# The head of a hybrid trunk's first mixer: three modulation sums on TensorE, a first group in halves, and projections whose sums stay in PSUM over two or three groups

## The chip, the cores and the metric

The kernel runs on one core of one Trainium2 chip. The metric is the device time of one execution in microseconds (us). Before the change three runs took 2713.58, 2715.54 and 2716.81; their median is 2715.54.

## The reference, cut to what matters

Two layers, 256 tokens, 2048 features, all in float32. The change touches the part from the input to the projections of layer 0's mixer:

```
c_act = silu(c)
mod   = c_act @ mod_w[layer] + mod_b[layer]        # 2048 x 12288 per layer
sh1, sc1, g1, sh2, sc2, g2 = split(mod, 6)
h     = rms_norm(x, norm_mix_w) * (1 + sc1) + sh1
proj  = h @ w_in                                   # layer 0: 2048 x 7184
gq, gk, gv, gz, gb, ga, aq, ak, av = split(proj)   # each 1024 wide, gb and ga 8
o_a = gated_deltanet(gq, gk, gv, gz, gb, ga, ...)  # causal conv of 4 taps and silu on q, k, v; l2 norm of q, k
o_b = chunk_band_attention(aq, ak, av, ...)        # rms norm of q and k per head
x   = x + g1 * (concat(o_a, o_b) @ w_out)          # then an MLP, then layer 1 (an SSD mixer and an MLP)
```

## The kernel before, in words

Activations lie feature-major in SBUF: 128 features on the partitions, 256 tokens along the free axis. The 2048 features are four groups `kg` of 4 x 128 rows. A weight chunk is 512 rows by 512 columns (1 MB), and a projection block is finished once its chunks of all four groups have been summed in PSUM.

A float32 product goes through TensorE in one of two ways. In a split chunk ScalarE rounds the weights to `wh` (L317) and VectorE takes the rest `wl` (L321), each in two halves of 128 x 1024, and each tile takes three fast products, wh·u_hi, wh·u_lo and wl·u_hi. In a whole chunk the raw float32 weights meet the float32 activations `hw` (L867); every such product stands as two records in the trace. Blocks that the gated delta rule uses (q, k, v: GQ, GK, GV, called q0, q1 and so on for the first and second 512 columns) have 256-column products with the weights stationary (`b_item`). Blocks for attention (AQ, AK, AV) have 512-column products with the activations stationary (`a_item`).

The head (L1543 to 1580) loads x, squares it on ScalarE, adds the squares on VectorE in eleven steps of 256 columns (L833), and gets the sum over features with ten one-column products against ones (20 records). Scale and shift of layer 0's first norm come from `mod_job`: one row of 128 outputs by 2048 inputs (1 MB) is loaded, and one VectorE instruction multiplies it with the broadcast silu(c) (`crow`) and sums it (L439). For the first group eight rows are needed, four feature blocks of 128 in both kinds. `norm_unit` then makes x·scale·R (`hf`, L862, VectorE), adds the shift and rounds (L864, ScalarE), and takes the rest (L865, VectorE).

Groups 0 to 2 each run eight chunks: k0 and q0, whose sums stay in PSUM banks (`pm`) over all groups, and v0, k1, q1, v1, aq, ak, whose sums leave PSUM after each group into SBUF (`partial`): copied by ScalarE in group 0 (L1590), added by VectorE in groups 1 and 2 (L1592). Meanwhile eight modulation rows per group go through VectorE. Group 3 runs k0, q0, the four chunks of AV, v0, the gates (`n_item`), and aq, ak, k1, q1, v1 whole; behind each block its convolution or head norm follows, and behind the gates the delta rule of the first heads (`gdn_group`) in small products that lie between the chunks. AQ+1, AK+1, AV+1, GZ and GZ+1 follow, four chunks each.

What sets the order: the program is written with short generator tasks. `tick` runs tasks between products by credits, `pump` issues modulation rows at `rate` per step, and a list scheduler of the framework then orders each engine's instructions by its own priorities, except where `keep_in_program_order` pins one. [...] All weight and modulation loads are issued by SyncE, in order, into four buffers of 1 MB (`rawp`); split halves have four buffers each (`wp`); units `up` are 18 of 4 KB per partition; PSUM has four single banks (`pm`) and two pairs (`pg`).

Of the kernel before, what the change touches and what calls it, by code (L numbers as in the profile page):

```python
# [112 lines left out]
class Trunk:  # L113
# [8 lines left out]
    def __init__(self, tc, ctx, ins, out):  # L122
# [7 lines left out]
        self.u_p = pool("up", 18)  # L130
# [9 lines left out]
        self.ahead = []  # L140
        self.pin_mod = 0
# [196 lines left out]
    def constants(self):  # L338
# [7 lines left out]
        cact = self.const([P, 16], "cact")  # L346
# [21 lines left out]
    def constants2(self):  # L368
# [3 lines left out]
        for n, f in (("gconv", 0.5), ("gnw", 0.5), ("sconv", 0.5), ("sconv_b", 0.5), ("qnw", P ** -0.5)):  # L372
            nc.vector.tensor_scalar(col(n), col(n), f, None, op0=ALU.mult)
# [50 lines left out]

    def mod_job(self, layer, vs, fs, step):


        nc = self.nc
        key = ("mix", layer) if vs[0] < 3 else ("mlp", layer)
        for f0 in range(fs.start, fs.stop, step):  # L430
            s = slice(f0, f0 + step)
            for f in range(f0, f0 + step):
                for v in vs:
                    t = self.mod[v % 3, key]
                    raw = self.raw_p.tile([P, 2048], F32, tag="raw", name=self.nm("mraw"))
                    nc.sync.dma_start(raw, self.i["mod"][layer, v, f])
                    yield
                    with self.priority(20):
                        x = nc.vector.scalar_tensor_tensor(raw, raw, 1.0, self.crow, op0=ALU.mult, op1=ALU.mult, accum_out=t[:, f : f + 1])  # L439
                    if self.pin_mod > 0:  # L440
                        self.pin_mod -= 1
                        self.tc.keep_in_program_order(x)
                    if f < s.stop - 1 or v != vs[-1]:
                        yield
            for v in vs:
                t = self.mod[v % 3, key][:, s]
                nc.vector.tensor_tensor(t, t, self.modb[:, layer, v, s], op=ALU.add)
                if v % 3 == 1:
                    nc.vector.scalar_tensor_tensor(t, t, 1.0, self.nw[key][:, s], op0=ALU.add, op1=ALU.mult)
                self.ready[v % 3, key] = f0 + step  # L450
# [22 lines left out]
    def loader(self, src, whole=False):  # L473
# [4 lines left out]
        res = []  # L478

        def load():  # L480
            raw = self.raw_p.tile([P, 2048], F32, tag="raw", name=self.nm("raw"))
            nc.sync.dma_start(raw, src)
            for hf in range(2):
                r = raw[:, 1024 * hf : 1024 * hf + 1024]
# [16 lines left out]
    def b_item(self, ps, src, act, first, last, after=None, whole=False):  # L501

        load, ws = self.loader(src, whole)

        def run():
            o_, (u, x) = ps(), act()
            for hf, (wh, wl) in enumerate(self.tiles(ws, 512)):
# [301 lines left out]
    def sumsq(self, cb, b, late=False):  # L809
# [3 lines left out]
        x = self.x[cb][:, 2 * b : 2 * b + 2]  # L813
        if cb == 3:
# [34 lines left out]
    def norm_unit(self, r, cb, key, acts, whole=False):  # L849
# [4 lines left out]
        x = []  # L854
        for b in range(2):
            h = self.s2([P, 2, SEQ], tag="hf")
            if whole:
                x.append(self.s2([P, 2, SEQ], tag="hw"))
            for f in range(2):
# [372 lines left out]
    def att_qk(self, ps, nw, part=None):  # L1232
# [19 lines left out]
        res = self.unit()  # L1252
# [284 lines left out]
    def run(self):  # L1537
# [274 lines left out]
```

## Time and profile before

| | us |
|---|---|
| median of the runs | 2715.54 |
| the profiled execution | 2719.37 |
| its span in the trace | 2717.6 |
| PE busy in the span | 2665.0 (98%) |
| DVE busy | 2147.6 (79%) |
| ACT busy | 1351.2 (50%) |

The profiled execution is 3.8 us above the median. PE is TensorE's matmuls, PEld its weight loads, DVE VectorE, ACT ScalarE, SP SyncE. A tile's name is given without its buffer number; `mraw` is a modulation row, `raw` a weight chunk, `u` a unit. Each row of a timeline gives start, duration, engine, source line, operation, output and inputs, shapes, count, and in brackets the idle time before it with what ended it.

### The profile page before, as it was taken

To read this page: it belongs to the slowest core of one execution; us is meant where nothing else is said; L and a number is where in the kernel's file an instruction comes from. 1 tells how busy PE (TensorE), PEld (TensorE's weight loads), DVE (VectorE), ACT (ScalarE), POOL (GpSimd) and SP (SyncE) were. 2 spreads that over 40 slices of the span, in tenths; PEclk is the share of its full clock that TensorE was granted. 3 is DMA by queue.
4 is the path that set the end of the run, shared out by engine and by line. 5 is a ranking of instruction groups with operands and counts; after the bars stand their busy time and mean duration, and the time that the engine had idled before them with its cause. 6 is when DMAs were issued, how large, how long until landed. Compare 5 with 4: busy or idle time off the path is not lost.

```text
span 2717.6 us, 39677 instructions
## 1 busy us (share of the span) xinstructions
PE 2665.0 (98%) x15664; PEld 2350.4 (86%) x15664; DVE 2147.6 (79%) x3081; ACT 1351.2 (50%) x1976; POOL 24.5 (1%) x98
## 2 busy tenths in 40 slices
PE   5999999999999999999999999999999999999999
PEld 5887989888888888888888888888888888888888
DVE  7998998987888888889889876897777855555554
ACT  3444454546445354454556544665555354454452
POOL 1000000000000000000000000000000000000000
PEclk9999999999999999999999999999999999999999
DMA  9986487867899898988456665554558855555554
GB/s 341 353 325 235 172 301 272 294 241 282 322 339 328 328 336 330 333 331 307 165 185 217 217 234 200 203 185 172 196 177 293 324 201 188 188 191 193 186 192 134
DMA packets 100459, 680.06 MB, mean 250 GB/s; under 512 B 11185, under 2 KB 14513, under 8 KB 19377
## 3 DMA queue, kind: packets, MB, share of 16 engines
q1 hardware_dynamic: 95376, 669.07, 68.5%
q10 hardware_dynamic: 4896, 8.46, 1.0%
q8 instruction: 123, 2.02, 0.3%
q14 instruction: 64, 0.52, 0.1%
HBM read 675.33 MB, written 2.16 MB: 249 GB/s over the span
## 4 chain that ended last, share of the span: by engine, by line
PE 90%; DVE 6%; DMA 1%; ACT 1%; issue 1%; SPq 0%; ACTq 0%; DVEq 0%
PE pw L308 70%; PE pg L308 13%; PE pm L311 4%; PE pm L308 3%; DVE mraw L439 2%; DVE wl L321 1%; PE pm L314 1%; DMA mraw<-in_mod_dram 1%; DVE u L1592 0%; ACT wh L317 0%; DVE hf L862 0%; ACT pm L1042 0%; DMA raw<-in_w_ab_dram 0%; DMA x<-in_x_dram 0%; DVE u L865 0%
## 5 line engine op out<-in xcount | busy, mean ns | idle before, releaser
L317 ACT CAST wh<-raw 128x1024 fp32r<-128x1024 f32 x870 | 907.1, 1051 | 1031.6 <-PE pw L308 732.9
L321 DVE TENSOR_TENSOR wl<-raw,wh 128x1024 fp32r<-128x1024 f32 x870 | 1048.7, 1220 | 463.8 <-ACT wh L317 349.6
L308 PE MATMUL pw<-u,wh 128*128 128x512 f32 x5584 | 1321.6, 391 | 2.6 <-DVE pad L973 1.9
L308 PEld LDWEIGHTS pw<-u,wh 128*128 128x128 f32 x5584 | 1032.2, 188 | 208.2 <-issue 3.3
L308 PEld LDWEIGHTS pw<-u,wl 128*128 128x128 f32 x5584 | 702.3, 191 | 21.3 <-issue 2.1
L308 PE MATMUL pw<-u,wl 128*128 128x256 f32 x5584 | 714.5, 283 | 0.3 <-DVE wl L321 0.3
L439 DVE SCALAR_TENSOR_TENSOR mraw<-mraw,crow 128x2048 f32<-128x2048 f32 x192 | 438.0, 2283 | 17.8 <-DMA mraw<-in_mod_dram 17.5
L308 PE MATMUL pg<-wh,u 128*128 128x512 f32 x864 | 281.6, 397 | 0.0
L308 PEld LDWEIGHTS pg<-wh,u 128*128 128x128 f32 x864 | 161.9, 188 | 32.1 <-issue 0.5
L925 DVE SCALAR_TENSOR_TENSOR x<-pw,mod,x 128x256 f32<-128x256 f32 x352 | 161.1, 478 | 22.6 <-PE pw L308 20.3
L308 PE MATMUL pg<-wl,u 128*128 128x512 f32 x432 | 169.9, 393 | 0.7 <-DVE wl L321 0.5
L308 PE MATMUL pg<-u,wh 128*128 128x256 f32 x672 | 124.6, 285 | 0.0
L308 PEld LDWEIGHTS pg<-u,wh 128*128 128x128 f32 x672 | 105.7, 192 | 0.3
L308 PEld LDWEIGHTS pg<-wl,u 128*128 128x128 f32 x432 | 81.4, 188 | 17.6 <-DVE wl L321 2.1
L308 PE MATMUL pg<-u,wl 128*128 128x256 f32 x336 | 95.3, 284 | 0.0
L308 PE MATMUL pm<-u,wh 128*128 128x256 f32 (+1 forms) x304 | 64.6, 310 | 19.2 <-ACT wh L317 19.2
L308 PEld LDWEIGHTS pm<-u,wh 128*128 128x128 f32 x304 | 49.1, 198 | 20.3 <-ACT wh L317 20.0
L308 PEld LDWEIGHTS pg<-u,wl 128*128 128x128 f32 x336 | 64.4, 192 | 0.1
L984 DVE SCALAR_TENSOR_TENSOR u<-pad,cst,u 128x256 f32<-128x256 f32 x144 | 60.6, 477 | 3.3 <-ACT u L978 3.2
L864 ACT ACTIVATE u<-hf,mod 128x256 fp32r<-128x256 f32 x64 | 29.3, 502 | 53.0 <-DVE hf L862 53.0
L1504 ACT ACTIVATE rl<-rs 128x512 f32<-128x512 f32 x64 | 40.4, 632 | 18.9 <-DVE rs L1499 14.4
L308 PE MATMUL pm<-u,wl 128*128 128x256 f32 x176 | 46.1, 290 | 3.1 <-DVE wl L321 3.1
(299 smaller groups left out, 1580.5 us busy)
## 6 DMA issues: line engine op xcount, KB each, us to landing
raw<-in_w_dram SPq DMA_DIRECT2D x256, 1024.0 KB, 5.0
mraw<-in_mod_dram SPq DMA_DIRECT2D x192, 1024.0 KB, 6.0
raw<-in_w_ab_dram SPq DMA_DIRECT2D x56, 1024.0 KB, 5.7
raw<-in_w_ssd_dram SPq DMA_DIRECT2D x48, 1024.0 KB, 4.9
raw<-in_w_sz_dram SPq DMA_DIRECT2D x32, 1024.0 KB, 4.9
raw<-in_wo_ssd_dram SPq DMA_DIRECT2D x32, 1024.0 KB, 4.8
raw<-in_wo_ab_dram SPq DMA_DIRECT2D x16, 1024.0 KB, 5.2
sE<-sd_rowd ACTq DMA_DIRECT2D x32, 256.0 KB, 4.9
```

Source lines behind the costliest of these rows:

```text
L308: self.nc.tensor.matmul(o, a, b, start=start, stop=stop, skip_group_check=True)
L311: self.nc.tensor.matmul(o, lhsT, rhs, start=True, stop=True, skip_group_check=True)
L314: self.nc.tensor.transpose(o, a, self.ident[:k, :k])
L317: a = self.nc.scalar.copy(hi, src)
L321: b = self.nc.vector.tensor_tensor(lo, src, hi.bitcast(F32), op=ALU.subtract)
L439: x = nc.vector.scalar_tensor_tensor(raw, raw, 1.0, self.crow, op0=ALU.mult, op1=ALU.mult, accum_out=t[:, f : f + 1])
L864: nc.scalar.activation(hi, h[:, f], AF.Identity, bias=shift[:, col])
L925: nc.vector.scalar_tensor_tensor(x[:, 2 * b + f], ps[:, f, n], g[:, 2 * cb + f : 2 * cb + f + 1], x[:, 2 * b + f], op0=ALU.mult, op1=ALU.add)
L984: nc.vector.scalar_tensor_tensor(h, pad[:, f, 1 + q : 257 + q], w[:, q, j : j + 1], h, op0=ALU.mult, op1=ALU.add)
L1504: nc.scalar.activation(rl, lo, AF.Relu)
```

## The change

Eight things change, all in the first mixer's part of `run` and in its helpers.

1. Three of the first eight modulation sums (shift and scale of feature group 0, shift of group 2) become TensorE products (`mod_pe`): the row arrives in another layout (a new input `mod0`, the same numbers), and 16 products of a 128 x 128 slice with one column of silu(c) give the 128 sums in a PSUM column of `sums`. `mod_fin` adds the bias from there. The other five stay on VectorE.
2. The squares are added in seven steps of 512 columns (L846), and four ones-products are left of ten.
3. `norm_first` replaces `norm_unit` for the mixer's norm: x·R over 512 columns on VectorE (L893), scale and shift in one ScalarE instruction per 256 columns (L902), then rounding and rest over 512 columns. The float32 result exists in every group, so any group can have whole chunks.
4. Group 0 begins in halves: the first half of k0 whole, then halves of q0, v0, k1 with the first half of the unit; the second halves follow once the modulation columns 2 and 3 are there. Half chunks are loaded into units, which are 19 instead of 18.
5. Instead of six blocks copied or added per group, each block's sums stay in PSUM for one, two or three groups, and are copied out once by ScalarE. The 24 VectorE additions of L1592 are gone; four additions come later, where a block's copied sum meets its last one.
6. The chunks are in another order (below). The chunks with k0's first half, aq of group 1, av of group 2 and k0 of group 3 become whole beside the five that were.
7. `rate` is 0.67, 0.57 and 0.57 instead of 0.5 in groups 0 to 2.
8. The head's loads and some small instructions are pinned in program order.

Order of the chunks before, with the group behind the @ and W for whole:

```
@0, @1, @2: k0 q0 v0 k1 q1 v1 aq ak
@3: k0 q0 | AV@0-3 | v0 | gates | aqW akW | (delta rule 0) | k1W | (attention 0) | q1W v1W | AQ+1@0-3 | (delta rule 1) | AK+1@0-3 ...
```

And now:

```
0: k0W(half) q0(half) v0(half) k1(half) | v0 k1 k0 q0 (second halves) | q1@0 v1@0 aq@0 ak@0
1: aqW@1 ak@1 k0@1 q0@1 av@0 av@1 aq1@0 aq1@1
2: avW@2 aq1@2 k0@2 q0@2 v0@1 v0@2 k1@1 k1@2
3: k0W q0 v0 | gates | k1W | aq@2 aqW@3 | (delta rule 0) | ak@2 akW@3 | av@3 | q1@1 q1@2 q1W@3 | (attention 0) | v1@1 v1@2 v1W@3 | aq1@3 | (delta rule 1) | AK+1@0-3 ...
```

```diff
+    def mod_pe(self, raw, o):
+        for k in range(16):
+            self.mmx(o, raw[:, k * P : k * P + P], self.cact[:, k : k + 1], k == 0, k == 15)
+
+    def mod_fin(self, layer, v, s, src=None):
+        key = ("mix", layer) if v < 3 else ("mlp", layer)
+        nc, t = self.nc, self.mod[v % 3, key][:, s]
+        a = nc.vector.tensor_tensor(t, t if src is None else src, self.modb[:, layer, v, s], op=ALU.add)
+        if self.in_order == 2:
+            self.tc.keep_in_program_order(a)
...
+    def norm_first(self, cb, key, acts, now=False):
+        nc = self.nc
+        scale, shift = self.mod[1, key], self.mod[0, key]
+        p, x = self.pair(), [self.s2([P, 2, SEQ], tag="hw") for _ in range(2)]
...
+            a = nc.vector.tensor_tensor(x[b], self.x[cb][:, 2 * b : 2 * b + 2], self.row(self.R, 2), op=ALU.mult)
...
+                nc.scalar.activation(x[b][:, f], x[b][:, f], AF.Identity, scale=scale[:, col], bias=shift[:, col])
+            self.split(x[b], p[b][:, :, 0], p[b][:, :, 1])
...
+        self.mod_pe(pe0, sums[:, 0:1])
...
+        self.mod_sum(dv0, 0, 0, 1)
+        r = self.norm_r()
+        self.pin_mod = 1
+        self.mod_sum(dv1, 0, 1, 1)
+        self.mod_pe(pe1, sums[:, 1:2])
+        nc.scalar.copy(self.R, self.norm_bc(r))
...
         def partial(n, ps):
-            first = parts[n] is None
-            if first:
-                parts[n] = self.unit(shape=[P, 2, 512])
+            parts[n] = self.unit(shape=[P, 2, 512])
             for b in range(2):
-                o = ps[b].rearrange("p f t -> p (f t)") if len(ps[b].shape) == 3 else ps[b]
-                if first:
-                    nc.scalar.copy(parts[n][:, b], o)
-                else:
-                    nc.vector.tensor_tensor(parts[n][:, b], o, parts[n][:, b], op=ALU.add)
+                nc.scalar.copy(parts[n][:, b], ps[b].rearrange("p f t -> p (f t)") if len(ps[b].shape) == 3 else ps[b])
...
+        chunk("k0", 0, True, (0,))
+        chunk("q0", 0, False, (0,))
+        self.mod_sum(dv[0], 0, 1, 2)
+        self.constants2()
+        self.mod_pe(pe2, sums[:, 2:3])
+        chunk("v0", 0, False, (0,))
+        dv = [self.mod_load(mod[0, v, 3]) for v in range(2)]
+        self.mod_fin(0, 0, slice(2, 3), sums[:, 2:3])
...
+        group(0, [("v0", 0, False), ("k1", 0, False), ("k0", 0, True), ("q0", 0, True),
+                  ("q1", 0, False), ("v1", 0, False), ("aq", 0, True), ("ak", 0, True)])
```

How this moves instructions, first on TensorE at the start. The rows are the engine's list in order; `ones,sq` are the sums of squares, `ident,rsy` the norm's broadcast, `cact,mraw` a modulation sum, `hw,u` the whole half of k0 (its weights are in a unit), `u,wh` and `u,wl` split products. Before:

```order
L308 MATMUL pm_163<-ones,ss 128x1 x2
L308 MATMUL pm_163<-ones,sq_162 128x1 x4
L308 MATMUL pm_163<-ones,sq_172 128x1 x4
L314 MATMUL pm_205<-ident,rsy_191 128x128 x2
L308 MATMUL pm_315<-u_289,wh_231 128x256 x2
L308 MATMUL pm_316<-u_289,wh_231 128x256 x2
L308 MATMUL pm_315<-u_289,wl_232 128x256
```

And of the changed kernel:

```order
L309 MATMUL pm_135<-cact,mraw_136 128x1 x16
L309 MATMUL pm_188<-ones,sq_185 128x1 x4
L309 MATMUL pm_135<-cact,mraw_144 128x1 x16
L315 MATMUL pm_227<-ident,rsy_196 128x128 x2
L309 MATMUL pm_299<-hw_233,u_236 128x256 x4
L309 MATMUL pm_300<-hw_233,u_236 128x256 x4
L309 MATMUL pm_135<-cact,mraw_289 128x1 x16
L309 MATMUL pm_341<-u_231,wh_295 128x256 x2
```

Two modulation sums stand ahead of the broadcast, and the third between the first and the second half chunk.

VectorE behind that third sum, in the changed kernel: `pm_135` is the PSUM tile of the three sums, wl_296 belongs to q0's half, wl_338 to v0's, wl_377 to k1's.

```order
L322 TENSOR_TENSOR wl_296<-u_293,wh_295 128x1024
L377 TENSOR_SCALAR cst<-cst 128x8
L377 TENSOR_SCALAR cst<-cst 128x64
L447 TENSOR_TENSOR mod_123<-pm_135,cst 128x1
L447 TENSOR_TENSOR mod_124<-mod_124,cst 128x1
L451 SCALAR_TENSOR_TENSOR mod_124<-mod_124,cst 128x1
L322 TENSOR_TENSOR wl_338<-u_335,wh_337 128x1024
L434 SCALAR_TENSOR_TENSOR mraw_367,mod_123<-mraw_367,crow 128x2048
```

The bias addition that reads the third sum stands ahead of v0's and k1's splits and of two more modulation rows.

TensorE in group 3, around the first delta rule's products. `gu` makes the decay matrices, `pm<-u` and `pm<-u,u` are small products of the convolved k and q, `hw,raw` and `raw,hw` are whole chunks, `wh,u` and `wl,u` split ones, `ident,…` transposes. Before (k1's whole chunk is pg_2568, q1's pg_2705):

```order
L311 MATMUL pm_2453<-gu_2411,SUmask 128x512
L314 MATMUL pm_2458<-ident,u_2154 128x128 x4
L314 MATMUL pm_2465<-ident,u_2154 128x128 x4
L311 MATMUL pm_2493<-u_1843 128x128 x4
L311 MATMUL pm_2506<-u_1843 128x128 x4
L311 MATMUL pm_2519<-u_1926,u_1843 128x128 x4
L308 MATMUL pg_2568<-hw_1718,raw_2339 128x256 x8
L308 MATMUL pg_2568<-hw_1728,raw_2339 128x256 x5
L311 MATMUL pm_2526<-u_1926,u_1843 128x128 x4
L308 MATMUL pg_2568<-hw_1728,raw_2339 128x256 x3
L308 MATMUL pg_2705<-hw_1718,raw_2560 128x256 x6
```

And of the changed kernel, where pg_2087 is ak and pg_2346 av:

```order
L312 MATMUL pm_2166<-gu_2128,SUmask 128x512
L315 MATMUL pm_2183<-ident,u_496 128x128 x4
L315 MATMUL pm_2190<-ident,u_496 128x128 x4
L312 MATMUL pm_2220<-u_1683 128x128 x4
L312 MATMUL pm_2233<-u_1683 128x128 x4
L309 MATMUL pg_2087<-raw_2085,hw_1313 128x512
L309 MATMUL pg_2346<-wh_2250,u_1310 128x512
L309 MATMUL pg_2346<-wl_2251,u_1310 128x512
```

Where a whole chunk followed the small products, a split one follows now, whose wl_2251 and wl_2255 VectorE makes inside the delta rule's chain.

## Rows read from the trace of the kernel before

**Rows 1.** The page: chain that ended last, by engine.

```profile
PE 90%; DVE 6%; DMA 1%; ACT 1%; issue 1%; SPq 0%; ACTq 0%; DVEq 0%
```

**Rows 2.** Stretches of the head, groups 0 to 2, and group 3's first two parts.

```profile
core 0: us, PE busy (x) PEld busy (x) DVE busy (x) ACT busy (x) POOL busy (x), PEclk, DMA share, GB/s
0.00:40.16 40.16, 8.71 (x38) 7.91 (x38) 29.06 (x60) 10.76 (x22) 8.33 (x38) 1.00 0.93 351
40.16:90.20 50.04, 48.29 (x337) 45.76 (x337) 40.97 (x49) 22.90 (x33) 0.00 (x0) 1.00 0.94 342
90.20:138.80 48.60, 46.95 (x341) 44.15 (x342) 46.89 (x56) 19.57 (x23) 0.00 (x0) 1.00 0.93 345
138.80:187.43 48.63, 46.48 (x336) 43.52 (x337) 47.61 (x60) 19.78 (x25) 0.00 (x0) 1.00 0.94 348
187.43:236.90 49.47, 49.47 (x286) 41.19 (x286) 47.74 (x74) 24.23 (x40) 0.62 (x6) 1.00 0.69 253
236.90:290.00 53.10, 52.34 (x306) 42.96 (x305) 46.56 (x152) 29.64 (x112) 3.42 (x10) 1.00 0.51 187
```

**Rows 3.** PE in order of time, the head.

```profile
5.50 3.65 PE L314 MATMUL pm<-ident,cact 128*128 128x128 f32 x16 [5.50 <-DVE cact L349]
...
22.03 0.66 PE L314 MATMUL pm<-ident,rsy 128*128 128x128 f32 x2 [6.63 <-DVE rsy L276]
40.16 1.22 PE L308 MATMUL pm<-u,wh 128*128 128x256 f32 x4 [17.47 <-ACT wh L317]
```

**Rows 4.** The chain in order of time: start, length, engine and line.

```profile
2.17 6.27 DMA x<-in_x_dram
9.19 0.47 ACT crow L358
11.01 4.41 PE pm L308 x20
...
30.89 4.43 DVE mraw L439 x4
...
89.10 1.04 ACT wh L317
90.16 1.24 DVE wl L321
```

**Rows 5.** Stretches whose records are of one kind (columns as rows 2).

```profile
11.01:15.40 4.39, 4.39 (x20) 4.31 (x20) 0.00 (x0) 0.71 (x2) 0.00 (x0) 1.00 1.02 426
40.16:45.21 5.05, 5.01 (x21) 4.72 (x22) 5.05 (x7) 3.43 (x6) 0.00 (x0) 1.00 0.81 290
45.21:60.00 14.79, 14.79 (x123) 14.79 (x123) 11.65 (x12) 4.20 (x4) 0.00 (x0) 1.00 1.00 351
198.57:220.36 21.79, 21.79 (x99) 18.03 (x97) 21.79 (x33) 11.66 (x18) 0.31 (x3) 1.00 0.60 205
427.80:431.30 3.50, 3.36 (x16) 3.39 (x17) 2.26 (x4) 1.65 (x3) 0.00 (x0) 0.51 0.95 365
```

**Rows 6.** PE later: whole chunks, a one-column product, two waits.

```profile
187.43 0.39 PE L308 MATMUL pm<-u,wl 128*128 128x256 f32 x1 [1.01 <-DVE wl L321]
229.75 7.03 PE L308 MATMUL pg<-raw,hw 128*128 128x512 f32 x16
245.88 4.05 PE L308 MATMUL pg<-hw,raw 128*128 128x256 f32 x18
575.16 0.50 PE L308 MATMUL pm<-ones,sq 128*128 128x1 f32 x4
427.94 1.09 PE L314 MATMUL pm<-ident,aq 128*128 128x128 f32 x4 [2.02 <-DVE aq L1250]
```

**Rows 7.** Groups of instructions from 40.16 to 187.43: busy, mean ns, idle before.

```profile
L321 DVE TENSOR_TENSOR wl<-raw,wh 128x1024 fp32r<-128x1024 f32 x49 | 57.9, 1219 | 9.9 <-ACT wh L317 9.5 <-issue 0.3
L439 DVE SCALAR_TENSOR_TENSOR mraw<-mraw,crow 128x2048 f32<-128x2048 f32 x24 | 54.8, 2282 | 0.2 <-DMA mraw<-in_mod_dram 0.2
L1592 DVE TENSOR_TENSOR u<-pg,u 128x512 f32<-128x512 f32 x22 | 14.3, 682 | 0.9 <-PE pg L308 0.9
L864 ACT ACTIVATE u<-hf,mod 128x256 fp32r<-128x256 f32 x13 | 6.5, 508 | 16.0 <-DVE hf L862 16.0
L447 DVE TENSOR_TENSOR mod<-mod,cst 128x2 f32<-128x2 f32 x12 | 1.9, 158 | 0.3
```

**Rows 8.** DVE in group 3: a filter step, a rest, the wait for norms.

```profile
192.69 2.45 DVE L959 SCALAR_TENSOR_TENSOR u<-pad,cst,u 128x256 f32<-128x256 f32 x6
254.53 0.17 DVE L1047 TENSOR_SCALAR gss<-gss 128x8 f32<-128x8 f32 x1 [0.72 <-ACT pm L1042]
```

More of the change, by code (lines that the diff above doesn't have):

```diff
@@ L499, in tiles, with b_item @@
         return [[w and w.rearrange("p (k c) -> p k c", c=width) for w in half] for half in ws]
-    def b_item(self, ps, src, act, first, last, after=None, whole=False):
-        load, ws = self.loader(src, whole)
+    def b_item(self, ps, src, act, first, last, after=None, whole=False, hfs=(0, 1)):
+        load, ws = self.loader(src, whole, hfs)
         def run():
             o_, (u, x) = ps(), act()
-            for hf, (wh, wl) in enumerate(self.tiles(ws, 512)):
+            for hf, (wh, wl) in zip(hfs, self.tiles(ws, 512)):
                 for ct in range(4):
@@ L1567, in run @@
+        self.mod_sum(dv1, 0, 1, 1)
+        self.mod_pe(pe1, sums[:, 1:2])
+        nc.scalar.copy(self.R, self.norm_bc(r))
         w = i["w_ab"]
         acts = []
-        mix0 = ("mix", 0)
-        nc.scalar.copy(self.R, r)
-        Task(self.norm_unit(self.R, 0, mix0, acts)).finish()
+        unit0 = Task(self.norm_first(0, mix0, acts, True))
+        unit0.step()
+        self.ahead.append(self.loader(w[0, GK], True, hfs=(0,)))
+        self.ahead[0][0].finish()
+        for v in range(2):
+            self.mod_fin(0, v, slice(0, 1), sums[:, v : v + 1])
@@ L1602, in last, with chunk @@
                              None if part is None else part.rearrange("p a (f t) -> p (a f) t", f=2))
-        def partial_item(kg, n, then=None):
+        def chunk(n, kg, whole=False, hfs=(0, 1), keep=True):
             c0, kind = kinds[n]
-            ps = held[n] if n < 2 else []
+            first = n not in banks
+            if first:
+                banks[n] = []
+            ps = banks[n]
             def psum():
-                if not ps and n < 2:
-                    ps.extend([self.pm([P, 2, SEQ]), self.pm([P, 2, SEQ])])
@@ new lines, in chunk, with group @@
+            if not keep:
+                del banks[n]
+            end = kg == 3 or not keep
+            if kind:
+                self.a_item(psum, w[kg, c0], lambda: unit_now(kg), first, end, after, whole)
+            else:
+                self.b_item(psum, w[kg, c0], lambda: unit_now(kg), first, end, after, whole, hfs)
+        def group(kg, seq):
+            self.modgen = self.mod_job(0, (0, 1), range(4 * kg + 4, 4 * kg + 8), 2)
+            unit = Task(self.norm_first(kg + 1, mix0, acts))
+            for n, (name, k, keep) in enumerate(seq):
+                chunk(name, k, n == 0 and kg > 0, (1,) if n < 4 and kg == 0 else (0, 1), keep)
+                if n == 3:
+                    unit.step()
+                if n == len(seq) - 2:
+                    self.pump(100)
+                    self.fast.append(unit)
```

225 lines of the change are left out of this document (141 added, 84 removed).

## The prediction

> **What bounds the kernel now.** First I read the chain of waits on the page: PE holds 90% of it and DVE 6% [rows 1]. What the change can win lies where PE isn't the chain, so I next asked for the busy time by stretches of the first mixer [rows 2]. Ahead of the first weight product, at 40.16 us, PE is busy for 8.71 us only. In groups 0 to 2 it is busy for all but 1.7 to 2.2 us of each, and in group 3 nearly all the time. The timeline of PE [rows 3] and the chain in order of time [rows 4] then say why the start is late: PE idles 17.47 us ahead of 40.16, and the chain runs through DVE's modulation rows, of which eight at 2.28 us are needed first. The other loss is in groups 0 to 2. They took 50.04, 48.60 and 48.63 us, 147.27 in all.
>
> What their products need comes from stretches of one kind [rows 5]. A 256-column product takes 14.79 / 123 = 0.120 us, so a split chunk of 48 takes 5.77. The four AV chunks (96 of the 99 records) take 21.79 / 4 = 5.45 each. Six of the one and two of the other are 45.5 a group, 136.5 for three; 10.8 us were lost. [...]
>
> **The start.** Before, the eight rows and the norm end at 40.16. Now PE can begin its first modulation sum when its own 16 transposes (to 9.15, rows 3) are done and ScalarE has copied `crow`, at 9.66 [rows 4]; its row is the first load. That all x now follows it is covered: x landed at 8.44 behind 2 MB, and 1 MB more takes 2.5 us at the 426 GB/s of 11.01 to 15.40 [rows 5], so the squares are done before the first sum ends; I let it cost nothing. A sum is 16 float32 products, two records each. At the start 20 one-column records took 4.41 us [rows 4], 0.22 each; the sum is 7.06 and ends at 16.7. The four ones-products (8 records) end at 18.5, the second sum at 25.5, the norm's two transposes (0.66, rows 3) at 26.2. The copy of R on ScalarE (as a 256-column instruction, 0.51) ends at 26.7, x·R (as the 512-column addition, 0.68) at 27.4, six small additions at 0.158 at 28.3, and scale and shift at 28.8 [rows 7]. The first product starts at 28.8 in place of 40.16: 11.4 us gained.
>
> **Products added ahead of group 3.** A whole chunk takes 7.03 us [rows 6] or, in 256 columns, 32 records of at most 4.05 / 18; I take 6.95 for both. k0's first half costs 3.5 in place of 2.9 (+0.6), aq@1 and av@2 cost 1.5 more each (+3.0). The third sum stands between half chunks on a warm engine, where four one-column records took 0.50 [rows 6]: 32 of them take 4.0 at most, I take 3.7. Four chunks of 5.45 replace four of 5.77 (-1.3). Sum: +6.0.
>
> **Group 0.** k0's half from 28.8 has 16 records: twelve fill the 5.05 slow us, four take 0.22, so it ends at 34.8; the third sum ends at 38.5. VectorE's list has the addition that reads this sum ahead of v0's and k1's splits and of ten rows, so they all wait for it. Behind it, up to the first split half of ak, stand 10 rows at 2.28, 13 halves at 1.22, four 512-column instructions at 0.68 and 11 small ones at 0.16: 43.2, or about 42 where neighbours overlap [rows 7]. ak can start at 80.5 and ends at 86.0. PE's own work would have ended at 28.8 + 6.0 + 3.7 + 42.6 = 81.1: a new wait of 4.9. The group ends 4.2 us earlier than before, where the start was 11.4 earlier.
>
> [...]
>
> **Groups 1 and 2.** The products are 45.7 and 47.0. VectorE has seven splits (17.1), eight rows (18.3) and 4.6 of the rest, 40 in all, since the 22 seen additions of 14.3 us are gone [rows 7]. The 8.3 of old waits should go; DVE is still at 85 to 88%, and I leave 1 us in each group (bounds: none, or the 3 of before). They end at 86.0 + 46.7 + 48.0 = 180.7. Before, group 3 effectively began two split chunks ahead of 198.57, at 187.0. So it begins 6.3 earlier.
>
> **Group 3.** k0 whole costs 1.2, and the four chunks that are 256-column ones now in place of AV's and AQ+1's cost 1.3: 3.8 us are left. Then the order. Before, the four AV chunks gave VectorE 21.8 us for the convolutions of k0 and q0, and whole chunks, which need no VectorE, filled the delta rule's gaps; in 236.90 to 290.00 PE was idle for 0.8 [rows 2]. Now k0, q0, v0 and k1 end within 29 us. A convolution is twelve filter steps of 0.41 [rows 8] and two or four additions, so VectorE falls behind, and the gates, the norm's 18 small steps (which began at 254.53, after 0.72 of waiting for ScalarE's squares) and av's halves stand in its list behind that. Walked step by step, PE waits 1.4 at aq@2 (the gates' copy stands on ScalarE behind a convolution's), 0.9 at the first decay product (which before also waited for the gates), 2.3 and 2.4 at av (its bank, then its second half) and about 5 in the delta rule's levels, where two splits stand between the small steps: 12, so up to 9 more than before. A walk hands on every delay whole, though; the nearest row, the 0.8 of the same chain before, is near none. Bounds 0 and 9, I take 2.5. Behind group 3 the same chunks stand in the same order, PE-bound.
>
> **Sum.** 11.4 - 6.0 - 4.9 + 8.3 - 2.0 = 6.8; counted by the groups' ends it is 6.3 (the waits are counted to 187.43, group 3's effective beginning is 187.0); - 2.5 for group 3's products, - 2.5 for its waits: 1.3 us gained. The profiled execution took 2719.37 around a span of 2717.6, 3.8 above the median 2715.54; I put the gain against the median: 2714. 0.2%, 5.4 us, is about what a measurement of this kernel tells from no change.
>
> **Rivals.**
> - *The waits don't come.* Group 3 loses nothing more (+2.5), groups 1 and 2 nothing (+2), and VectorE's chain in group 0 runs 2 us shorter. For it: 0.8 us idle in the old chain; against it: DVE busy for 47 of 49 us there. Gain 7.8: 2708, down to 2703.
> [...]
> - *The third sum runs slow.* [...] At 7.06 in place of 3.7, with VectorE held, group 0 ends 3.4 later: 2717.
> - *The transfers set the pace*, so that the dropped additions win nothing: groups 1 and 2 take 48.6 again, as at 345 GB/s with DMA at 0.94 [rows 2]. Against it: 426 GB/s were moved from 11.01 to 15.40 [rows 5]. 2.5 less: 2717.
>
> **How the numbers follow.** Forecast 0.35 (own range 2709 to 2719; 0.08 of it faster, 0.02 slower); no waits 0.32 (0.28 faster); backlog 0.16 (0.13 slower); slow third sum 0.11 and transfers 0.06 (0.15 the same, 0.02 slower). Faster 0.36, same 0.47, slower 0.17. The range reaches into the second and third case: 2703 to 2724.
>
> **What would show it.** Right: PE's first weight product at 28 to 30 us, group 0's last split on DVE back to back from about 38, group 3's first product at 179 to 182, no L1592 additions on DVE, and PE idle 2 to 6 us more than before from there to the second delta rule. Wrong: a start beyond 32 (a load is late), the third sum at 7 us, groups 1 and 2 at 48 us, or pauses over 2 us with a clock of 0.5 in group 3; or, on the other side, a group 0 without a wait.

## The result, and the profile after

The changed kernel takes 2722.73 us (median of 8 executions, 2722.48 to 2726.90), the kernel before 2715.68 (8, 2713.58 to 2720.74): ratio 1.0027, interval 1.0016 to 1.0038. It is slower, by 7.0 us at the medians; forecast was 2714.0, 1.5 faster. The profiled execution took 2723.6 with a span of 2721.8. The profile shown of before has a pause of its own at 427.94 [rows 6]; where group 3 is compared, the profile of before_u19 (the first experiment, the kernel before with one buffer more) stands for it, with a span of 2715.8. The two profiles are 6.0 us apart, the medians 7.0.

The head, PE in order of time (start, length, engine, line, operation, idle before and what ended it), answers to [rows 3]:

```profile
6.81 3.29 PE L315 MATMUL pm<-ident,cact 128*128 128x128 f32 x16 [6.81 <-DVE cact L350]
10.04 4.31 PE L309 MATMUL pm<-cact,mraw 128*128 128x1 f32 x32
14.87 1.86 PE L309 MATMUL pm<-ones,sq 128*128 128x1 f32 x8 [0.51 <-DVE sq L846]
16.59 6.97 PE L309 MATMUL pm<-cact,mraw 128*128 128x1 f32 x32
23.42 0.67 PE L315 MATMUL pm<-ident,rsy 128*128 128x128 f32 x2
26.24 5.60 PE L309 MATMUL pm<-hw,u 128*128 128x256 f32 x16 [2.15 <-ACT hw L902]
31.68 3.63 PE L309 MATMUL pm<-cact,mraw 128*128 128x1 f32 x32
```

The first weight product starts at 26.24 in place of 40.16, and the third sum takes 3.63. But 13.9 us at the start are hardly any at the end of group 0. VectorE, from there on, shows why:

```profile
35.34 0.16 DVE L447 TENSOR_TENSOR mod<-pm,cst 128x1 f32<-128x1 f32 x1 [3.27 <-PE pm L309]
...
50.98 1.23 DVE L322 TENSOR_TENSOR wl<-u,wh 128x1024 fp32r<-128x1024 f32 x1 [2.23 <-ACT wh L318]
...
70.23 2.36 DVE L322 TENSOR_TENSOR wl<-u,wh 128x1024 fp32r<-128x1024 f32 x2 [1.68 <-ACT wh L318]
...
80.01 1.21 DVE L322 TENSOR_TENSOR wl<-u,wh 128x1024 fp32r<-128x1024 f32 x1
```

It waits for the third sum until 35.34 and then works its list down to ak's first split, which ends at 81.22. PE has to wait for that one, and then runs slowly:

```profile
81.28 0.79 PE L309 MATMUL pg<-wl,u 128*128 128x512 f32 x1 [2.17 <-DVE wl L322]
81.87 1.05 PE L309 MATMUL pg<-wh,u 128*128 128x512 f32 x2
...
85.26 0.62 PE L309 MATMUL pg<-wh,u 128*128 128x512 f32 x2
```

```profile
81.28:85.03 3.75, 3.75 (x10) 2.98 (x11) 3.07 (x4) 3.61 (x5) 0.00 (x0) 0.54 1.01 423
```

In that stretch (columns as [rows 2]) 0.54 is granted behind the idle 2.17 us: two records take 1.05 there and 0.62 from 85.26, and the nine up to 85.03, at 0.42 each in place of 0.23, lose 1.7 us. Behind the 1.71 us that PE idles up to 43.11, 1.00 is granted (43.11 to 46.00).

The stretches (columns as [rows 2]): the head, groups 0, 1 and 2, then three parts of group 3.

```profile
0.00:26.24 26.24, 16.77 (x91) 16.13 (x91) 13.27 (x33) 8.84 (x17) 7.44 (x38) 0.75 0.94 376
26.24:88.24 62.00, 55.98 (x360) 51.59 (x361) 52.57 (x68) 27.07 (x38) 0.00 (x0) 0.91 0.98 389
88.24:134.05 45.81, 45.81 (x234) 37.07 (x233) 37.44 (x42) 19.17 (x24) 0.00 (x0) 1.00 0.86 331
134.05:182.48 48.43, 47.37 (x329) 42.18 (x328) 36.18 (x39) 19.15 (x24) 0.00 (x0) 1.00 0.88 339
212.00:260.00 48.00, 43.91 (x199) 29.94 (x200) 44.01 (x126) 25.72 (x87) 2.31 (x6) 1.00 0.63 230
260.00:300.00 40.00, 40.00 (x344) 39.48 (x344) 25.89 (x54) 14.34 (x32) 4.20 (x8) 1.00 0.38 135
340.00:392.00 52.00, 49.49 (x254) 40.35 (x253) 51.72 (x110) 27.67 (x86) 2.77 (x7) 1.00 0.81 309
```

Group 0 ends at 88.24 (before: 90.20), groups 1 and 2 take 94.2 us (97.2), and group 3 starts at 182.48; in before_u19 it effectively starts at 187.58 (two split chunks of 5.76 ahead of its AV chunks), so 5.1 are won. In group 3 PE idles 4.09 of 48 us at 212 to 260 and 2.51 of 52 at 340 to 392, where VectorE is busy for 51.72; in between, at 260 to 300, VectorE idles for 14. Before, it was busy there all the time, as the line below shows. But a busy VectorE is no proof by itself: at 340 to 392 it was busy for 50.14 of 52 us before, and PE idled 0.79 only.

```profile
260.00:300.00 40.00, 39.81 (x278) 36.67 (x277) 39.73 (x107) 17.03 (x38) 4.07 (x12) 1.00 0.42 147
```

What PE waited for in group 3, up to the first output product (line, waited for: us in total, times, longest); after:

```profile
PE pg L309 <- DVE wl L322: 2.7, 3, 1.2
PE pg L309 <- ACT pg L1299: 1.5, 1, 1.5
PE pg L309 <- ACT wh L318: 1.0, 1, 1.0
```

and in before_u19:

```profile
PE pm L314 <- DVE aq L1250: 1.4, 2, 0.8
PE pm L311 <- DVE gvn L1147: 1.0, 1, 1.0
PE pm L308 <- DVE wl L321: 1.0, 1, 1.0
```

Before, PE waited for results of the delta rule and the norms, a little; now it waits for weights that VectorE hasn't split and for a bank that ScalarE hasn't emptied. Over the whole stretch up to the first output product:

```profile
182.48:492.96 310.48, 302.59 (x2048) 269.32 (x2047) 268.21 (x567) 150.32 (x386) 14.39 (x38) 1.00 0.65 238
```

and in before_u19:

```profile
187.58:489.50 301.92, 297.85 (x1962) 263.32 (x1963) 273.04 (x571) 155.28 (x394) 13.95 (x38) 1.00 0.68 248
```

It is 8.6 us longer: 3.8 more idle (7.9 against 4.1) and 4.7 more busy. By the usual distance between records of each shape, 2.4 is products: 144 more records of 0.120 us and 32 more of 0.216, and 96 fewer of 0.227. The other 6.2 are losses (some 14 against 8 in all), part of them inside records that count as busy. At the first output product the changed kernel is 3.5 behind, and at PE's last record 5.9. The other 2.4 come in layer 1, some 890 us further on, in part from loads of `sE`:

```profile
1392.15 0.34 ACTq L1429 DMA_DIRECT2D sE<-sd_rowd  x1
1392.53 1.34 ACTq L1429 DMA_DIRECT2D sE<-sd_rowd  x1
...
1399.52 0.69 DVE L1455 TENSOR_TENSOR sE<-sE,sd_col 128x512 f32<-128x512 f32 x1 [2.54 <-DMA sE<-sd_rowd]
...
1400.87 0.44 PE L315 MATMUL pm<-ident,u 128*128 128x128 f32 x2 [1.83 <-DVE u L1042]
```

Before:

```profile
1390.29 0.34 ACTq L1370 DMA_DIRECT2D sE<-sd_rowd  x1
1390.66 0.45 ACTq L1370 DMA_DIRECT2D sE<-sd_rowd  x1
...
1395.56 0.69 DVE L1396 TENSOR_TENSOR sE<-sE,sd_col 128x512 f32<-128x512 f32 x1 [1.33 <-DMA sE<-sd_rowd]
```

The same loads, in the same order of instructions, but the second one's issue takes 1.34 in place of 0.45, VectorE waits 2.54 in place of 1.33 for a load, and PE pauses 1.83.

That isn't all of it. PE, in the stretch behind a pause of 1.91 us that both kernels have, and in the one behind the 1.83 us (columns as [rows 2]); after:

```profile
1381.64:1385.09 3.45, 3.45 (x9) 2.68 (x9) 3.45 (x10) 0.99 (x2) 0.00 (x0) 0.52 0.33 76
1400.87:1405.56 4.69, 4.69 (x20) 4.04 (x21) 4.69 (x7) 3.87 (x7) 0.00 (x0) 0.65 0.23 44
```

and the same products in before_u19:

```profile
1378.54:1380.47 1.93, 1.93 (x8) 1.58 (x9) 1.93 (x6) 0.99 (x2) 0.00 (x0) 1.00 0.00 0
1394.58:1397.75 3.17, 3.17 (x20) 2.77 (x20) 3.17 (x5) 2.85 (x5) 0.00 (x0) 1.00 0.23 87
```

The changed kernel is 3.1 behind at the first, 4.6 behind its end, 6.3 at the second and 7.8 behind that; by 1644 it has won back 1.9. So the wait for the load is 1.7, and the lower clock behind the two pauses 1.5 each. The first of these isn't the change's: the profile of before has it too, 0.50 granted from 1380.18 to 1383.20, behind 1.91 us of idling.

### The profile page after: what moved, and what is told of

Same layout as the page of the kernel before. It is cut to its first block, busy times and chain, and to the rows that moved or that the text cites. A ratio compares the mean times of both kernels' runs of the same rounds, so it can differ in the third digit from the quotient of the medians.

```text
span 2721.8 us, 39725 instructions
## 1 busy us (share of the span) xinstructions
PE 2684.8 (99%) x15708; PEld 2361.7 (87%) x15708; DVE 2118.5 (78%) x3034; ACT 1348.1 (50%) x1971; POOL 24.1 (1%) x98
## 3 DMA queue, kind: packets, MB, share of 16 engines
q8 instruction: 123, 2.02, 0.3%
## 4 chain that ended last, share of the span: by engine, by line
PE 91%; DVE 5%; ACT 2%; issue 1%; DMA 1%; SPq 0%; ACTq 0%; DVEq 0%
PE pw L309 71%; PE pg L309 13%; PE pm L312 4%; PE pm L309 3%; DVE wl L322 1%; DVE mraw L434 1%; PE pm L315 1%; DVE u L1014 1%; ACT wh L318 0%; ACT pm L1097 0%; DMA raw<-in_w_ab_dram 0%; DMA sE<-sd_rowd 0%; DMA x<-in_x_dram 0%; ACT pg L1299 0%; DVE u L1017 0%
## 5 line engine op out<-in xcount | busy, mean ns | idle before, releaser
L322 DVE TENSOR_TENSOR wl<-raw,wh 128x1024 fp32r<-128x1024 f32 x834 | 1006.3, 1220 | 464.7 <-ACT wh L318 351.6
L318 ACT CAST wh<-raw 128x1024 fp32r<-128x1024 f32 x834 | 870.7, 1051 | 986.8 <-PE pw L309 722.0
L434 DVE SCALAR_TENSOR_TENSOR mraw<-mraw,crow 128x2048 f32<-128x2048 f32 x189 | 431.2, 2283 | 14.8 <-DMA mraw<-in_mod_dram 14.6
L309 PE MATMUL pg<-wh,u 128*128 128x512 f32 x832 | 272.5, 400 | 3.4 <-ACT pg L1299 1.5
L309 PE MATMUL pg<-wl,u 128*128 128x512 f32 x416 | 164.4, 395 | 4.9 <-DVE wl L322 4.9
L309 PE MATMUL pm<-u,wh 128*128 128x256 f32 (+1 forms) x256 | 54.3, 307 | 0.0
L1558 DVE TENSOR_TENSOR rs<-pw,rs 128x512 f32<-128x512 f32 x64 | 43.7, 683 | 4.7 <-ACT rs L1557 4.7
L1557 ACT COPY rs<-pw 128x512 f32<-128x512 f32 x64 | 36.9, 576 | 17.3 <-PE pw L309 17.3
L322 DVE TENSOR_TENSOR u<-rl,u 128x512 fp32r<-128x512 f32 x64 | 43.8, 685 | 0.0
```

The costliest lines, as they stand in the source:

```text
L309: self.nc.tensor.matmul(o, a, b, start=start, stop=stop, skip_group_check=True)
L318: a = self.nc.scalar.copy(hi, src)
L322: b = self.nc.vector.tensor_tensor(lo, src, hi.bitcast(F32), op=ALU.subtract)
L434: x = self.nc.vector.scalar_tensor_tensor(raw, raw, 1.0, self.crow, op0=ALU.mult, op1=ALU.mult, accum_out=self.mod[v % 3, key][:, f : f + 1])
L1557: nc.scalar.copy(lo, ps[:, :, 1])
L1558: nc.vector.tensor_tensor(lo, ps[:, :, 0], lo, op=ALU.add)
```

## The experiments

All were timed against the kernel before on the same chip (its medians there: 2714.5 to 2715.4). The changed kernel was timed on two chips, at ratios of 1.0027 and 1.0032, so differences of 1 to 2 us between experiments tell nothing. Theory M puts the whole loss inside the first mixer, where the prediction has its terms; the others are named in the expectations.

**after_again.** The changed kernel once more: 2725.20, ratio 1.0032 (1.0020 to 1.0043). Expected were the same waits in group 3 and the late load in layer 1. Both came: waits of 0.86 at 213.40, 1.53 at 247.60 and 1.20 at 252.03, and the second load of `sE` issued in 1.47.

**before_u19.** The kernel before with the 19th unit buffer.

```
-        self.u_p = pool("up", 18)
+        self.u_p = pool("up", 19)
```

> The kernel before with 19 units in the unit pool in place of 18, and nothing else: every engine's list of instructions is the same, only the buffers that units lie in (and so the places where one waits for another's buffer) differ, in the whole program. Theory M (the loss is made inside the first mixer, by its products and its order): no change, ratio 1.000 within 0.001, near 2715.7 us. Rival D (part of the loss comes from behind the mixer, where the profile of the changed kernel lost 2.2 us more in layer 1 and the median 3 more than the profile shows, because units lie elsewhere): 2 to 5 us slower, 2718 to 2721.

2715.74; ratio 1.0002 (0.9993 to 1.0010). The buffer alone does nothing.

**head_only and groups_only.** The new head with groups 0 to 3 in the old order, with the additions through SBUF; and the old head with the new groups.

```
 # head_only, in place of group(1, ...), group(2, ...) and the new order of group 3
+for kg in (1, 2): group(kg, [k0, q0 kept; v0, k1, q1, v1, aq, ak not kept])
 ...
 # groups_only: group 0 begins as before
+group(0, [("k0", 0, True), ("q0", 0, True), ("v0", 0, False), ("k1", 0, False), ("q1", 0, False), ...])
```

> The new head (three sums as products, squares in seven steps, the norm in 512-column steps, the first group's first four chunks in halves), but groups 0 to 3 with the chunks, additions through VectorE and whole chunks of before. Theory M: first product at 26.2 us as in the changed kernel; group 0 ends about 88, groups 1 and 2 take 48.6 each, so group 3 starts at 185.5 in place of 187.0 and then runs as before: 1 to 2 us faster than before, 2714. Rival H (the head itself costs what it wins, through the third sum and the waits it makes): group 0 ends at 90 or later and the time is 2716 to 2719. Rival D adds 2 to 5 to either.

> The head of before (eight sums on VectorE, no halves), with the changed kernel's groups 0 to 3: sums held in PSUM, its order of chunks and its whole chunks. Theory M: groups 1 and 2 take 94.2 us together in place of 97.2, group 3 up to the first output product 310.5 in place of 304.2, so 3 us slower than before, 2719, and most of the 7 us of loss. Rival H: the groups gain and the head loses, 2713 or less. Rival D adds 2 to 5 to either.

head_only: 2719.79, ratio 1.0015 (1.0006 to 1.0024). Its first product comes at 26.73, and it wins nothing, where theory M gave 2714: a miss. Its groups 0, 1 and 2:

```profile
26.60:88.61 62.01, 55.86 (x360) 51.50 (x361) 51.42 (x66) 28.18 (x41) 0.00 (x0) 0.91 0.90 354
88.61:139.15 50.54, 47.37 (x338) 44.63 (x336) 46.62 (x54) 21.58 (x25) 0.00 (x0) 0.97 0.91 344
139.15:189.70 50.55, 47.38 (x337) 44.63 (x336) 45.44 (x53) 19.83 (x22) 0.00 (x0) 0.97 0.90 333
```

Group 0 takes 62 us where it took 50.04 [rows 2], and groups 1 and 2 lose 1.9 each on before, with a clock of 0.97. What makes groups 1 and 2 slower there is open. groups_only: 2722.98, ratio 1.0029 (1.0019 to 1.0038), as slow as the whole change and 4 us above what theory M gave:

```profile
40.00:88.95 48.95, 47.22 (x334) 44.91 (x333) 42.38 (x52) 23.41 (x31) 0.00 (x0) 0.96 1.00 404
88.95:182.35 93.40, 92.89 (x561) 79.16 (x560) 75.29 (x81) 38.36 (x48) 0.00 (x0) 1.00 0.86 334
182.35:493.26 310.91, 302.71 (x2048) 269.38 (x2046) 268.47 (x567) 150.35 (x386) 14.41 (x38) 1.00 0.65 238
```

With the old head group 0 ends at 88.95, with the new one at 88.24: the earlier start is worth 0.7 there. Group 3 is as long as in the changed kernel without the new head. The profile shown is the fastest execution of groups_only, 1.8 us below its median, and is 3.8 behind before_u19 at the first output product and 3.7 at PE's last record; what the slower executions add is not shown.

**late_fin.** The addition that reads the third sum is pinned behind v0's half split and two rows.

```
+        self.pin, self.pin_mod, self.in_order = 1, 2, 2
 ...
+        for v in range(2):
+            self.mod_sum(dv[v], 0, v, 3)
         self.mod_fin(0, 0, slice(2, 3), sums[:, 2:3])
 ...
```

> The changed kernel with the bias addition that reads the third TensorE sum moved behind v0's first half split and the two modulation rows of feature block 3 (all pinned in that order); nothing left out. Theory V (VectorE's hold of 3.3 us up to 35.3 is what ak's wait of 2.2 us and the half clock behind it, 1.7, come from): VectorE's list runs 3.3 us earlier, ak's wait goes, 3 to 4 us faster than the changed kernel, 2719. Rival A (ScalarE binds there: VectorE's waits of 2.2 and 1.7 us for casts that stand behind PSUM copies grow instead): at most 1 us faster, 2722.

2724.06, ratio 1.0024 (1.0015 to 1.0033). The first sum took 6.91 in its profile, the first product came at 28.59, and group 0 ended at 89.84: it took 61.3 us, 0.7 less than in the changed kernel, so the 3.27 us for which VectorE is held there are not what decides. A miss for the prediction's sentence on them, and theory V with it. Of the two waits for casts that rival A names, the first grew from 2.23 us to

```profile
52.59 1.23 DVE L322 TENSOR_TENSOR wl<-u,wh 128x1024 fp32r<-128x1024 f32 x1 [4.75 <-ACT wh L318]
```

On ScalarE that cast stands behind the copy of a finished sum, which waits for PE. So VectorE's list starts late there for two reasons, and taking away one brings out the other.

**rows_later and rows_catch.** No background row from group 3's start until av; then the old rate, or one that makes the four rows good.

```
-        self.rate, self.rate2 = 0.25, 1.1
+        self.rate, self.rate2 = 0.0, 1.1
 ...
         chunk("av", 3)
+        self.rate = 0.25      # rows_catch: 0.52
```

> The changed kernel with no modulation rows issued from group 3's first chunk until av's chunk; they follow at the usual pace later. Theory B (VectorE's backlog from four convolutions and from rows of 2.28 us each is what the delta rule's chain waits behind): four rows, 9 us, leave that stretch, the waits from 211 to 258 us (5.6) fall to 2 or less, 3 to 4 us faster than the changed kernel, 2719. Rival S (the waits are ScalarE's and the chain's own length: gates copied behind a convolution's tanh, squares, a bank released by ScalarE): they fall by 1 us at most and the time stays within 1 us of the changed kernel.

> Edit: no modulation row of the background is issued from group 3's start until av's chunk (rate 0 in place of 0.25, about four rows of 2.28 us fewer on VectorE there), and the rate is 0.52 from av's chunk to aq@1's so that the four are made up before the second delta rule. The whole computation. Theory B (VectorE's backlog in the first 60 us of group 3 is what PE waits for at 246 to 258): the losses of 240 to 260 fall from 5.3 to about 1.4 us as in rows_later, nothing is missing at 560 to 600, and the time is about 4 below the changed kernel's 2722.7 to 2725.2: 2719 to 2721. Rival G (VectorE has no slack anywhere between group 3's start and the first output product, so that what is taken from it early is paid as a wait later): first output product at 493 to 496 as before, time 2722 to 2727.

rows_later: 2738.83, ratio 1.0081 (1.0069 to 1.0093). At 240 to 260 PE is busy for 19.41 us in place of 16.40, but at 560 to 600 the rows come too late:

```profile
240.00:260.00 20.00, 19.41 (x110) 14.72 (x110) 19.64 (x45) 8.58 (x27) 2.10 (x4) 1.00 0.48 168
560.00:600.00 40.00, 30.28 (x155) 26.33 (x154) 32.10 (x42) 11.35 (x13) 0.00 (x0) 0.83 0.89 334
```

The early waits went, as theory B said, but the time is far outside both ranges. rows_catch keeps the early gain (19.21 us) without that, and takes 2723.53, ratio 1.0030 (1.0019 to 1.0042). In its profile the first output product comes 1.4 earlier than in the changed kernel's; the times show no gain. Rival G, that what is taken off early is waited for later, is nearer.

**aq_early and catch_aq.** aq's two chunks stand ahead of v0, where the AV chunks stood, and the first delta rule starts behind ak; catch_aq is this with rows_catch and ak's first chunk whole.

```
+        for kg in (2, 3):
+            chunk("aq", kg, kg == 3)
         chunk("v0", 3)
 ...
```

> Edit: in group 3 the two chunks of aq stand ahead of v0 and the gates (as the four AV chunks did in the kernel before), and the first delta rule is started behind ak instead of behind aq. The same work in another order. Theory B: VectorE has about 13 us with one split chunk only for the convolutions of k0 and q0, the waits of 244 to 258 fall by 3 to 4 us, and the time is 2719 to 2721. Rival G: the delta rule begins some 10 us later with fewer products left beside it, its levels wait instead, time 2722 to 2728. If the time is above 2728, the place of the first delta rule, not the backlog ahead of it, sets the first mixer's end.

> Edit: rows_catch and aq_early together, and ak's chunk of group 0 without a split (as in ak_whole). The whole computation. Theory B: the gains add, 4 from the rows, 2 more from the order, up to 1 from ak: 2715 to 2718, level with the kernel before. Rival G: 2721 to 2728, since VectorE's work until the first output product is the same.

aq_early: 2735.43, ratio 1.0077 (1.0063 to 1.0090): 10 to 13 us worse than the changed kernel. In the beginning of group 3 PE is busy for 31.31 of 36.71 us, and in the second delta rule for 36.43 of 40 (380 to 420):

```profile
183.29:220.00 36.71, 31.31 (x167) 26.05 (x166) 31.49 (x56) 15.50 (x28) 0.93 (x7) 0.95 0.62 219
```

A miss: moving cover is no gain in itself. catch_aq, 2723.98, ratio 1.0034 (1.0022 to 1.0047), missed theory B's 2715 to 2718 too and is in rival G's range. With its rows held back, and ak whole, the same place of the first delta rule costs 11 us less than in aq_early. So that place alone, which the expectation of aq_early would blame above 2728, isn't what lost them.

**short_g0.** From the second chunk of group 0 to its end each VectorE sum covers 64 of 2048 columns, so most of each of these sums is left out.

```
 ...
+            n = 64 if self.short else 2048
-            x = ...(raw, raw, 1.0, self.crow, ...)
+            x = ...(raw[:, :n], raw[:, :n], 1.0, self.crow[:, :n], ...)
```

> Edit: in the changed kernel the VectorE sums of group 0 alone (the rows of f 2 and 3, and group 0's eight background rows) cover 64 of 2048 columns, about 22 us of VectorE's work less there. Theory V0 (VectorE's list sets group 0's end, so the earlier first product is not passed on): group 0 ends at 81 to 83 in place of 88 to 89, group 3 starts at 176 to 178, time 2717 to 2719. Rival (ScalarE's casts and copies, the banks or the transfers hold it): group 0 ends at 86 or later, time 2721 to 2725. If group 0 ends early and the time doesn't fall, group 3 or what is behind it gives the gain back.

2716.54, ratio 1.0006 (0.9997 to 1.0015): 6 us of the 7 are back. Group 0 and groups 1 and 2:

```profile
26.30:82.48 56.18, 55.59 (x360) 52.10 (x361) 30.31 (x67) 27.05 (x38) 0.00 (x0) 0.89 0.99 404
82.48:175.92 93.44, 92.93 (x562) 79.21 (x560) 73.23 (x80) 38.36 (x48) 0.00 (x0) 1.00 0.89 351
```

PE idles 0.6 us, and group 0 ends at 82.48, the end that the prediction gave for PE's own work being 81.1. So the time of VectorE's rows is what holds group 0, as the expectation said; the transfers are the same. The gain arrives whole at the end. Even so the kernel isn't faster than before.

**short_g3 and before_short.** The same cut from group 3's start to the first output product, in either kernel.

```
+        self.short = True     # at group 3's start; False ahead of the output blocks
```

> Edit: from group 3's start to the first output product each of the 37 modulation sums on VectorE covers 64 of its 2048 columns (the values are then not the reference's; transfers and counts of instructions stay), so some 80 us of VectorE's work there are gone. Theory B (backlog on VectorE is what PE waits for in group 3): the losses from group 3's start to the first output product fall from 14.2 to about 6, the first output product starts at 485 to 487, time 2713 to 2717. Rival O (the order of the products alone: a level of the delta rule waits for its neighbours whatever VectorE has to do): losses still 11 or more, time 2719 to 2725.

> Edit: the same cut in the kernel before (sums over 64 of 2048 columns in group 3 alone). Theory B: its losses there, 8.1, fall to about 5, time 2711 to 2714, and the changed kernel's short_g3 is then within 4 of it. Rival O: it gains 3 to 5 as well, but short_g3 stays 6 or more above it.

short_g3: 2721.10, ratio 1.0024 (1.0015 to 1.0032); before_short: 2716.12, ratio 1.0003 (0.9994 to 1.0012). The stretch to the first output product in the one

```profile
182.82:490.22 307.40, 302.63 (x2056) 270.46 (x2055) 207.43 (x569) 151.86 (x388) 14.28 (x38) 1.00 0.66 241
```

and in the other:

```profile
186.81:490.03 303.22, 299.08 (x1970) 264.54 (x1971) 211.07 (x575) 155.50 (x396) 14.02 (x38) 1.00 0.68 247
```

With some 62 us less on VectorE the kernel before idles as much as ever (4.1), so nothing there waited for its rows. The changed kernel idles 4.8 in place of 7.9: 3.1 of its 3.8 extra us of idle time, and of the 6.2 us of losses, go with VectorE's rows. At the median that is 1.6 us, inside the intervals. Theory B's 2713 to 2717 is missed, and so are both theories' gains for before_short; short_g3's time is in rival O's range. 4.2 us of difference between the two stretches stay, 2.4 of them products. What the rest of the losses comes from is open.

**ak_whole, two_whole.** To relieve VectorE in group 0 at a price on PE: ak's first chunk whole; aq's and ak's whole, with rows_catch.

```
-                chunk(name, k, n == 0 and kg > 0, ...)
+                chunk(name, k, n == 0 and kg > 0 or kg == 0 and name in ("aq", "ak"), ...)  # ak_whole: "ak" alone
```

> The changed kernel with ak's chunk of group 0 whole too: 1.5 us more of products, and VectorE and ScalarE have one chunk less to split before group 1. Theory V (VectorE's list sets the end of group 0, and ak's wait of 2.2 us lowers the clock, 1.7 more): both go, the group ends 2.4 us earlier, near 85.9, and the time is 2 us below the changed kernel. Rival A (ScalarE's casts bind and the wait moves to aq or to group 1's second chunk): no change or 1.5 slower.

> Edit: rows_catch, and aq and ak of group 0 in whole products (as k0 is), four splits of 1.22 us fewer on VectorE there, 2.5 us more on PE. The whole computation. If VectorE's list sets group 0's end and the products are covered: group 0 ends at 85 to 86 in place of 88 to 89, group 3 starts near 179, time 2718 to 2721, still above the kernel before (layer 1's 2 to 3 us and group 3's products are left). Rival (what is saved in group 0 is waited for in group 3 again): 2722 to 2726.

2722.44, ratio 1.0023 (1.0014 to 1.0032), and 2721.02, ratio 1.0020 (1.0011 to 1.0029): the lowest median of a whole computation with the change, by less than the intervals, and still above the kernel before. The earlier group 3 that both expectations wanted did not come: in the profiles it starts at 182.28 and 183.37, against 182.48. (rows_ak, rows_later with ak whole, took 2734.94, ratio 1.0073, where 2716 to 2724 was expected.)

**after_408 and before_409.** Whether the late load in layer 1 goes with the number of transfers that SP's queue issued before: one weight chunk of group 1 in one transfer; sixteen loads of layer 0's MLP in halves.

```
+            if (n, kg) == ("aq1", 1):
+                self.in_units = False
```

> Edit: in the changed kernel one weight chunk (aq@1's second head, the last of group 1) is loaded by one transfer in place of two halves, so SP's queue has issued 408 transfers in place of 409 at the loads of sE in layer 1. Theory Q (the position on the queue decides): the second load of sE is issued in 0.45 us in place of 1.34, lands 5 us after its issue in place of 7, and the time falls by 2 to 3, to 2719.5 to 2722. Rival (timing or where the data lie, not the count): the load still lands 7 us after its issue, time 2722.5 to 2725.5.

> Edit: in the kernel before sixteen weight loads of layer 0's MLP are each issued as two halves, so SP's queue has issued 409 transfers in place of 393 at the loads of sE in layer 1. Theory Q: the second load of sE is issued in 1.0 to 1.6 us and lands 7 us after its issue, time 2717 to 2719. Rival: as before, 2714 to 2716.5.

2724.97, ratio 1.0040 (1.0027 to 1.0053), its second load still issued in 1.12; and 2714.71, ratio 1.0002 (0.9993 to 1.0011), issued in 0.45. Theory Q falls on both sides.

## Why the prediction was wrong

- **The start** was right or better: 26.24 against 28.8, since 32 one-column records took 4.31 and 6.97 where 7.06 was taken for each. The third sum took 3.63 (3.7).
- **Group 0**: end 88.24 against 86.0. That VectorE's list decides was right (short_g0). That v0's split and the rows behind it wait for the addition was the author's estimate: VectorE idled 3.27 us ahead of the addition at 35.34, and that split began at 35.68. The third sum ended 3.3 earlier than forecast, but the chain from there to ak's first split was 45.9 us, not 42, since VectorE waited there for ScalarE's casts (2.23 and 1.68), and the 0.54 granted behind PE's pause of 2.17 us cost another 1.7. The walk had counted VectorE's instructions alone. Some 2.2 late. For k0's half the forecast took 5.05 slow us from the row at 40.16 [rows 5], an estimate; the half took 5.60 where 6.0 was added, its first nine records 3.92 with 0.51 granted (26.24 to 30.16). That the third sum's end alone sets the list's pace was wrong: with the hold gone, the wait for the cast grew to 4.75 (late_fin).
- **Groups 1 and 2**: 94.2 against 94.7; right. No run shows the 8.3 us of old waits in the forecast's sum, an estimate of the author's: PE idled 1.75, 1.65 and 2.15 us in groups 0 to 2 before [rows 2], and 0.00 and 1.06 in groups 1 and 2 of the changed kernel. The start of group 3 is 5.1 earlier, 6.3 was predicted.
- **Group 3's products**: +2.4 against +2.5; right.
- **Group 3's extra waits** is the step that failed, a term mis-sized: "Bounds 0 and 9, I take 2.5". Measured 6.2. The walk had the places (aq@2: 0.86 at 212.50; av: 1.52 for its bank, 1.19 for its second half), and I threw most of it away for a row of before, 0.8 idle. In that row VectorE was busy for 46.56 of 53.10 us beside PE, and for 39.73 of 40 from 260 to 300; in the new order it has nothing to do for 14 of these 40. So the row said nothing of the new order. 3.1 of the 6.2 us go with VectorE's rows (short_g3); the rest is open. The backlog rival (0.16) named the direction and the place, and the measured time lies in its 2721 to 2726, but in part by luck. It had 9 us of extra waits and 5 of clock pauses in group 3, the latter an estimate from one pause of before (0.51 granted behind 2.02 us at 427.94 [rows 5], [rows 6]); 1.00 was granted in each of the stretches of group 3, also behind the wait of 1.52 at av (246.68 to 250.00), and 2.4 us came in layer 1, where it had none.
- **Behind group 3** I put it at nothing, since the same chunks stand there in the same order. 2.4 more are lost there: in layer 1 a late load of `sE` and the lower clock behind two pauses, less what is won back. One of the pauses is the kernel before's as well, so part of the 2.4 is a difference between executions. The slow issue of the load (1.34 us in the changed kernel, 1.35 in late_fin, 0.45 in before) is in all profiles of kernels with both the new head and the new groups but one (two_whole: 0.45), and in none of before, before_u19, before_short, before_409, head_only or groups_only. Its cause stays open: the instructions there are identical, and the count of transfers isn't it.

From the forecast's -1.3 to the measured +5.9 at PE's last record: 1.2 at group 3's start, -0.1 of products, 3.7 of waits, 2.4 behind group 3, 7.2 in all.

## What to carry to other kernels

An earlier start is worth what the busiest other engine lets through: walk that engine's list to the end of the stretch, with its own waits for the casts it reads, before counting the start as won. When an order changes, idle time measured in the old order is no evidence for the new; look at where the second engine was busy beside the first, and whether that overlap survives. If a walk step by step names places and sizes, don't discount it by a row of another order: of the 9 us that this one gave, 6.2 came, not 2.5.

## What the runs showed of the hardware

- One-column float32 products: 32 records took 4.31, 6.97 and 3.63 us in the same execution. The stretches of the three sums in the changed kernel (columns as [rows 2]):

```profile
10.04:14.35 4.31, 4.31 (x33) 4.23 (x32) 2.80 (x5) 3.49 (x7) 0.00 (x0) 0.85 1.02 431
16.59:23.40 6.81, 6.81 (x33) 6.81 (x34) 4.45 (x16) 0.00 (x0) 0.00 (x0) 0.50 1.00 403
31.68:35.17 3.49, 3.49 (x34) 3.49 (x32) 0.40 (x3) 0.00 (x0) 0.00 (x0) 1.00 0.92 379
```

  PE is busy without a gap in each, and was granted 0.85, 0.50 and 1.00. The second stands behind 40 such records, the third behind 16 of 256 columns. In late_fin, two_whole, after_again, after_408 and rows_catch the first sum took 6.91, 6.91, 4.04, 6.82 and 3.86 us, the second 6.96 or 6.97, and the third 3.63, 4.79, 4.52, 3.63 and 3.63. In after_again, with PE busy without a gap from 26.83, the pairs of 256-column records behind the third sum took 0.63 each up to 41.33 and 0.40 from 42.49.
- Ahead of the same product in layer 1 PE idles 1.91 us in the profiles of the changed kernel and of before_u19; behind it 0.52 was granted in the changed kernel (1381.64 to 1385.09) and 1.00 in the other (1378.54 to 1380.47). In group 0 of the changed kernel 1.00 was granted behind 1.71 us of idling (43.11 to 46.00), 0.55 behind 1.88 (60.39 to 64.22).
- The issue of the second load of `sE` on ScalarE's queue took 0.45 us in before, before_u19, groups_only and two_whole, 1.34 in the changed kernel and 1.35 in late_fin, with the same instructions around it. The load landed 4.9 us after its issue in before and 7.0 in the changed kernel.
